# A hybrid encoder block on one core: a chain of constant products ahead of the first loop, and nine gate stores moved to another DMA queue

## The chip, the core and the metric

The kernel runs on one core of a Trainium2 chip. The metric is the device time of one execution in microseconds (us), as the median of several runs. The core has five engines that run side by side and wait for each other through semaphores: TensorE (PE in the profile; PEld is its weight load), VectorE (DVE), ScalarE (ACT), GpSimd (POOL) and SyncE (SP). Here SP does nothing but issue DMA transfers; ACT and POOL issue some too. Each engine takes its instructions strictly in the order in which the program lists them, so an instruction that waits holds up everything behind it on its engine.

## What is computed

One layer of a streaming encoder, in float32, for 16 meta tokens and 1024 positions of width 1024:

```python
xn = rmsnorm(h, norm_mix_g)
q, k, v, f_logit, u, gates = split(xn @ w_in)          # widths 512, 512, 512, 8, 512, 2048
y_a = forgetting_attention(q, k, v, f_logit) @ w_attn_out
z = gelu(s5(u))                                        # complex diagonal state-space model, 32 groups
zg = z @ w_glu
y_s = zg[..., :1024] * sigmoid(zg[..., 1024:])
g = sigmoid(gates)
h = h + (g[..., :1024] * y_a + g[..., 1024:] * y_s) @ w_o
h = h + conv_ffn(rmsnorm(h, norm_ffn_g))               # 1024 -> 5632 -> conv width 3 -> gated -> 1024
out = rmsnorm(h, norm_final_g)[16:]
```

## The kernel before

Every large product is made of three products of a reduced-precision format: each operand is cut into a high part (a cast, `hi`) and a low part (the rest, `lo`), and hi*hi, lo*hi and hi*lo are summed in one PSUM bank. A weight chunk therefore goes through a load (`raw`), a cast on ACT (`whi`) and a low part, which for the gate chunks is made by an ACT copy of the negated high part and a POOL DMA that adds the original to it in place (`wlo`, line 144).

The part of the program that matters here is its first 200 us:

1. **The first loop** (lines 405 to 413). The 1040 positions are cut into four blocks of 272, 256, 256 and 256. For block 0 the features (`xa` to `xhi`, `xlo`, lines 383 and 384) and the weights of `u` (`uraw` to `uh`, `ul`, lines 409 and 137) arrive in six pieces; as each arrives, TensorE adds its products to four PSUM banks, one for each 128 columns of `u`: 8 x 4 x 3 = 96 matmuls of 128x272 in all, on lines 351 to 353. The banks come from a ring of three called `mm` and a single one called `po`, so that the fifth product asked for, the first of block 1, gets the bank of the first:

```python
def mm_ps():
    mm_n[0] += 1
    if mm_n[1] and mm_n[0] % 4 == 0:
        return po_ps()
    return pp.tile([P, 512], F, tag="mm", name="mm", bufs=3)
```

   It is free once ACT has copied the first product out (line 421). Blocks 1 to 3 follow, 96 matmuls of 128x256 each.
2. **The state-space stage**, about 60 to 180 us. `u` is written to DRAM in another layout (`u_d`, line 455, 32 stores on SP's and POOL's queues) and read back by quarters (`U`, line 1910: quarters 0 and 1 on SP's queue, 2 and 3 on ACT's). For each quarter: tables `Vm` and `Gm` on DVE; transposes of `Vm` into `Wi` (PE line 1903, copied by ACT on line 1904); the input products `Wi` x `U` (PE line 1916, copied to `wr` and `wi` by eight ACT copies on lines 1919 and 1920); a scan on DVE into `St`; small products `Kt` (PE line 1879, ACT line 1881), spread to `Tm` by eight SP transfers (line 1889); the output products with `St` and `Tm` (PE lines 1957 and 1959), which ACT copies to `Y` (line 1960). There are two buffers for `U`, so that the load of quarter 3 follows the output products of quarter 1.
3. **The gate chunks**, in the same stretch. Eight chunks of 128 gate channels (i = 8 to 15, KD is 8), each in three pieces of 342 positions of 24 matmuls of 128x342 (lines 170 to 172), fill TensorE between the steps of the state-space stage. Below, 9.2 is the third piece (2) of chunk 9. ACT makes each piece a sigmoid (`gs`, line 505) and the piece is stored to DRAM (`g_d`, line 506). Chunk 8 has a buffer of its own (`g0s`); the others take turns in two buffers, so the sigmoid of a piece waits until the store of the piece two before it has landed:

```python
if i == KD:
    gs = g0s[:, t:t + n]
else:
    gs = pl.tile([P, LQ // 3], F, tag="gs", name="gs", bufs=2)
S.activation(gs, ps[:, :n], AF.Sigmoid)
GP.dma_start(g_d[P * i:P * i + P, t:t + n], gs)
```

   The stores stand on POOL's queue, in line with the loads of the gate weights and the `wlo` transfers. Since the buffers lie where `usb` (the rows of `u`) lay, the first sigmoid of chunk 9 also waits for the `u_d` stores.

Behind these stages come the key and query projections, the gated linear unit, the attention, the output projection and the feed-forward network, to 1440 us.

The order of instructions on each engine isn't written by hand: the code lists the steps, and a scheduler orders them when the program is built, by a model of their durations. An instruction added anywhere shifts that model's clock, and with it the order of independent steps behind it.

Of the kernel before, what the change touches and what calls it, by code (L numbers as in the profile page):

```python
# [9 lines left out]
F = mybir.dt.float32  # L10
# [9 lines left out]
P = 128  # L20
D = 1024
KD = D // P
# [22 lines left out]
UN = UBLK[0][1]  # L45
# [13 lines left out]
def block_kernel(ctx, tc, x, meta, xbt, x0t, g1t, w_q, w_k, w_v, w_f, w_u, w_g, b_f, w_ao, lam_d, bw_d, cw_d,  # L59
# [5 lines left out]
    V, S, GP, PE, SY = nc.vector, nc.scalar, nc.gpsimd, nc.tensor, nc.sync  # L65
# [13 lines left out]
# [5 lines that stand above are left out]
# [13 lines left out]
    def t_ps(name="tp"):  # L97
        return pp.tile([P, 512], F, tag="tp", name=name, bufs=2)
# [10 lines left out]
    g_d = dp.tile([2 * D, LQ], F, name="g_d")  # L109
# [36 lines left out]
    def wchunk(src, k, eng=None, act=False, copy=False):  # L146
        raw = wp.tile([P, k, P], F, tag="raw", name="raw", padded_shape=[P, KD, P])
        ld = (GP if act else SY).dma_start(raw, src)
        if act:
            after(ld, late[0])  # L150
        hi = wp.tile([P, k, P], R, tag="whi", name="whi", padded_shape=[P, KD, P])
        lo = wp.tile([P, k, P], R, tag="wlo", name="wlo", padded_shape=[P, KD, P])
        if act:
            cast = S.copy(hi, raw)
            if n_act[0]:
                after(cast, late[1])
            n_act[0] += 1
            lo_by_dma(lo, hi, src)
            return hi, lo
        if copy:  # L160
            S.copy(hi, raw)
            split_lo(V, lo, raw, hi)
            return hi, lo
        GP.tensor_scalar(hi, raw, 1.0, 0.0, ALU.mult, ALU.add)
        split_lo(eng or V, lo, raw, hi)
        return hi, lo

    def dense_steps(ps, whi, wlo, ahi, alo, k):
        for i in range(k):
            yield PE.matmul(ps, whi[:, i, :], ahi[:, i], start=(i == 0), stop=False)  # L170
            yield PE.matmul(ps, whi[:, i, :], alo[:, i], start=False, stop=False)  # L171
            yield PE.matmul(ps, wlo[:, i, :], ahi[:, i], start=False, stop=(i == k - 1))  # L172
# [126 lines left out]
    uraw = [wp.tile([P, 2, SW], F, tag="raw", name="uraw") for _ in range(2)]  # L299
    uraw += [sp.tile([P, 2, SW], F, tag="Tm", name="uraw", bufs=2) for _ in range(2)]  # L300
    uh = [wp.tile([P, 2, SW], R, tag=tag, name="uh") for tag in ("whi", "wlo") for _ in range(2)]
    xm = sp.tile([META, D], F, tag="tq", name="xm", bufs=3)

    xT = {0: [sp.tile([P, 4, UN], F, tag="tq", name="xa", bufs=3) for _ in range(2)]}
# [185 lines left out]
    def gate_chunk(i, pl, tanh):  # L490
        whi, wlo = gate0[1:] if i == KD else wchunk(w_g[i], KD, GP, act=not tanh)
        if tanh:
            gs = pl.tile([P, LQ], F, tag="gs", name="gs", bufs=1)
        for t, n in QBLK[::-1] if i == KD else QBLK:
            ps = mm_ps()
            yield from dense_steps(ps[:, :n], whi, wlo, xhi[:, :, T0 + t:T0 + t + n],
                                   xlo[:, :, T0 + t:T0 + t + n], KD)
            if tanh:
                S.activation(gs[:, t:t + n], ps[:, :n], AF.Tanh, scale=0.5)
# [3 lines that stand above are left out]
                else:  # L503
                    gs = pl.tile([P, LQ // 3], F, tag="gs", name="gs", bufs=2)
                S.activation(gs, ps[:, :n], AF.Sigmoid)
                GP.dma_start(g_d[P * i:P * i + P, t:t + n], gs)
        if tanh:
            GP.tensor_scalar(gs, gs, 0.5, 0.5, ALU.mult, ALU.add)
            if pl is not gp_ and i == KD - 1:
                okeep["g"] = gs  # L510
            else:
                SY.dma_start(g_d[P * i:P * i + P], gs)

    def stage_gates():
        for i in range(KD, 2 * KD):
            yield from gate_chunk(i, gp_, False)
# [412 lines left out]
    for pr in range(H // 2):  # L929
# [11 lines left out]
        for i in range(done, done + GA[pr]):  # L941
            gens.append(gate_chunk(i, ap, True))
            cnt += GAN
# [121 lines left out]
    for mm in gate_chunk(KD - 1, mg, True):  # L1065
        tc.add_manual_dep(mm.ins, marks[-1].ins.name, mybir.DependencyInfo(
            mybir.DependencyClass.NoSync, mybir.DependencyReason.DATA), reason="reserve")
# [959 lines left out]
```

## Time and profile before

| | us |
|---|---|
| Median of 3 runs | 1443.2 (1442.69 to 1445.39) |
| The profiled execution, time | 1445.58 |
| Its span in the trace | 1443.8 |
| TensorE busy in the span | 1422.4 (99%) |
| DVE, ACT, POOL busy | 1074.5, 722.4, 766.9 |
| Bytes moved by DMA | 214.06 MB |

The profile gives times from the start of the span. In a row of the timeline stand the start, the duration, the engine, the line, the operation, and output<-input with shapes; in brackets the idle time before it and what ended that. In a row of the waits stand the waiting instruction, what it waited for, and the total, the number and the longest of the waits. In a row of the windows stand the stretch, its length, and for each engine its busy time with the number of instructions. A busy TensorE isn't one at full speed: a matmul that is issued at half the rate still counts as busy.

### The profile page before, as it was taken

What the parts mean: (1) busy time and instruction counts of PE and PEld (TensorE: products, weight loads), DVE (VectorE), ACT (ScalarE), POOL (GpSimd) and SP (SyncE); (2) the same over time, 40 slices, a digit from 0 to 9 for tenths busy, and PEclk for the clock granted to TensorE, in tenths of its full rate; (3) what the DMA queues carried; (4) which work ended last, traced back from release to release, by engine and by line L of the source; (5) the groups of instructions that cost most, each with busy time, mean ns of one, the idle gap of its engine ahead of it and who ended that gap; (6) DMA issues with size and microseconds to landing.
All of it is one profiled execution on the core that took longest, in us unless ns stands there. A gap on an engine that the chain in (4) does not pass through costs nothing. (4 is left out here: it accounts for less than half of the span.)

```text
span 1443.8 us, 26609 instructions
## 1 busy us (share of the span) xinstructions
PE 1422.4 (99%) x9655; PEld 1346.2 (93%) x9655; DVE 1074.5 (74%) x2203; ACT 722.4 (50%) x1419; POOL 766.9 (53%) x887
## 2 busy tenths in 40 slices
PE   8999999999999999999999999999999999999997
PEld 8999999988999999999879999999999999887886
DVE  7999788843657676656469987788877776788875
ACT  7646585423646565533646444444444445643433
POOL 2642258632456556415861335555555544887794
PEclk9999999999999999999999999999999999999999
DMA  8675644521147422167964156667753327964333
GB/s 297 177 180 164 156 108 148 154 96 30 38 139 162 123 63 71 41 230 245 261 154 138 63 132 173 170 166 186 190 139 112 99 79 253 330 203 145 111 87 117
DMA packets 92968, 214.06 MB, mean 148 GB/s; under 512 B 15090, under 2 KB 22898, under 8 KB 92452
## 3 DMA queue, kind: packets, MB, share of 16 engines
q1 hardware_dynamic: 73124, 166.32, 35.0%
q0 software_dynamic: 17696, 41.29, 15.0%
q10 hardware_dynamic: 2016, 4.74, 0.9%
q8 instruction: 76, 1.25, 0.4%
q14 instruction: 56, 0.46, 0.1%
HBM read 170.88 MB, written 71.71 MB: 168 GB/s over the span
## 5 line engine op out<-in xcount | busy, mean ns | idle before, releaser
L170 PE MATMUL mm<-xhi,whi 128*128 128x342 f32 (+2 forms) x480 | 156.9, 327 | 1.3 <-DVE q L137 1.0
L172 PE MATMUL mm<-xhi,wlo 128*128 128x342 f32 (+2 forms) x480 | 155.3, 324 | 0.0
L171 PE MATMUL mm<-xlo,whi 128*128 128x342 f32 (+2 forms) x480 | 155.2, 324 | 0.0
L1183 POOL TENSOR_TENSOR ov<-ov,og 128x1024 f32<-128x1024 f32 x21 | 50.8, 2419 | 118.2 <-ACT og L1182 115.9
L137 DVE TENSOR_TENSOR sw<-sf,sw 128x512 fp32r<-128x512 f32 x72 | 74.2, 1031 | 46.2 <-ACT sw L1174 45.2
L1174 ACT CAST sw<-sf 128x512 fp32r<-128x512 f32 x72 | 44.9, 623 | 109.0 <-POOL sf L1321 80.2
L170 PEld LDWEIGHTS mm<-xhi,whi 128*128 128x128 f32 x480 | 90.5, 188 | 2.7 <-PE sp L818 0.8
L172 PEld LDWEIGHTS mm<-xhi,wlo 128*128 128x128 f32 x480 | 90.3, 188 | 0.6 <-issue 0.2
L171 PEld LDWEIGHTS mm<-xlo,whi 128*128 128x128 f32 x480 | 90.4, 188 | 0.2
L867 ACT CAST th<-tp 128x256 fp32r<-128x256 f32 (+3 forms) x120 | 56.2, 472 | 61.5 <-PE tp L860 29.3
L137 DVE TENSOR_TENSOR tl<-tp,th 128x256 fp32r<-128x256 f32 (+3 forms) x120 | 65.1, 547 | 25.7 <-ACT th L867 24.2
L1321 POOL TENSOR_TENSOR sf<-raw,sf 128x512 f32<-128x512 f32 x36 | 62.5, 1736 | 38.6 <-DVE sw L137 38.5
L1321 POOL TENSOR_TENSOR sf<-raw 128x512 f32<-128x512 f32 x36 | 48.5, 1348 | 62.2 <-DVE sw L137 23.4
L234 PE MATMUL mm<-xhi,sw 128*128 128x258 f32 (+1 forms) x288 | 81.0, 281 | 0.0
L232 PE MATMUL mm<-xhi,sw 128*128 128x258 f32 (+1 forms) x288 | 80.8, 280 | 0.0
L233 PE MATMUL mm<-xlo,sw 128*128 128x258 f32 (+1 forms) x288 | 80.7, 280 | 0.0
L832 POOL TENSOR_SCALAR pt<-pt,nm 128x144 f32<-128x144 f32 (+4 forms) x72 | 52.5, 742 | 49.3 <-DVE nm L831 48.2
L1373 DVE SCALAR_TENSOR_TENSOR ov<-hv,cwt,ov 128x1024 f32<-128x1024 f32 x36 | 69.0, 1918 | 0.4 <-ACT ov L1371 0.4
L1174 ACT CAST sw<-raw 128x512 fp32r<-128x512 f32 x70 | 43.0, 620 | 47.7 <-PE sp L234 23.9
L830 ACT ACTIVATE pt<-pt,nm 128x144 f32<-128x144 f32 (+4 forms) x72 | 52.9, 736 | 26.8 <-DVE nm L829 26.4
L823 DVE CUSTOM_DVE_ANT_0 pt<-sp,fb 128x328 f32<-128x328 f32 (+8 forms) x112 | 46.4, 430 | 20.1 <-PE sp L818 11.3
L137 DVE TENSOR_TENSOR sw<-raw,sw 128x512 fp32r<-128x512 f32 x70 | 57.4, 823 | 4.9 <-ACT sw L1174 4.7
(722 smaller groups left out, 5726.9 us busy)
## 6 DMA issues: line engine op xcount, KB each, us to landing
raw<-in_w_up_dram SPq DMA_DIRECT2D x44, 512.0 KB, 3.7
t_d<-in_w_dn_dram POOLq DMA_DIRECT2D x44, 256.0 KB, 6.9
wr<-t_d SPq DMA_DIRECT2D x44, 256.0 KB, 3.7
ar<-a_d SPq DMA_DIRECT2D x41, 256.0 KB, 5.1
a_d<-ov SPq DMA_DIRECT2D x18, 512.0 KB, 2.6
wr<-in_w_dn_dram SPq DMA_DIRECT2D x33, 256.0 KB, 3.7
t_d<-in_w_dn_dram SPq DMA_DIRECT2D x22, 256.0 KB, 4.4
t_d<-t_d SPq DMA_DIRECT2D x22, 256.0 KB, 4.8
```

The costliest lines, as they stand in the source:

```text
L137: return eng.tensor_tensor(out_, src, hi.bitcast(F), ALU.subtract)
L170: yield PE.matmul(ps, whi[:, i, :], ahi[:, i], start=(i == 0), stop=False)
L171: yield PE.matmul(ps, whi[:, i, :], alo[:, i], start=False, stop=False)
L172: yield PE.matmul(ps, wlo[:, i, :], ahi[:, i], start=False, stop=(i == k - 1))
L232: PE.matmul(ps, a[0][:, i], bh, start=(i == 0 and not joins), stop=False, skip_group_check=True)
L233: PE.matmul(ps, a[0][:, i], bl, start=False, stop=False, skip_group_check=True)
L234: PE.matmul(ps, a[1][:, i], bh, start=False, stop=(i == kh - 1), skip_group_check=True)
L830: S.activation(pt[:n, :kc], pt[:n, :kc], AF.Exp, bias=nm[:n, 1:2], scale=0.125, accum_out=nm[:n, 2:3])
L867: S.copy(th[:kn, z:tw], tp[:kn, z:tw])
L1174: S.copy(hi, src)
L1321: sums.append(GP.tensor_tensor(f_, a, b, op))
L1373: V.scalar_tensor_tensor(out=o, in0=h_[:, j:SEQ + j], scalar=cwc(j, m), in1=o, op0=ALU.mult, op1=ALU.add)
```

## The change

Two edits. First, ahead of the loads, DVE fills 128x272 numbers of a weight buffer that isn't needed yet (`uh[3]`, the last of the four `uh` buffers) with ones, and TensorE multiplies that tile by itself 17 times, into a PSUM bank of the ring `tp`. Nothing reads the result. The buffer's later writer, the cast of the last `uraw` piece, waits for these products. Second, the stores of chunks 8, 9 and 10, nine pieces, are issued by SP and no longer by POOL.

```diff
     uh = [wp.tile([P, 2, SW], R, tag=tag, name="uh") for tag in ("whi", "wlo") for _ in range(2)]
+    V.memset(uh[3].bitcast(F)[:, 0, :UN], 1.0)
+    busy = t_ps("busy")
+    for _ in range(17):
+        PE.matmul(busy[:, :UN], uh[3][:, 0, :P], uh[3][:, 0, :UN], start=True, stop=True)
     xm = sp.tile([META, D], F, tag="tq", name="xm", bufs=3)
...
                 S.activation(gs, ps[:, :n], AF.Sigmoid)
-                GP.dma_start(g_d[P * i:P * i + P, t:t + n], gs)
+                (SY if i < KD + 3 else GP).dma_start(g_d[P * i:P * i + P, t:t + n], gs)
```

Line numbers behind 301 are higher by 4 in the changed kernel. The order of the instructions differs from the first loop on to the forget gate's products (lines 537 and 538 before, 180 to 190 us); behind them it is the same on all engines.

SP's queue, from the stores of `u_d` on. Before:

```order
L455 DMA u_d<-usb 16x8x130 x16
L1910 DMA U<-u_d 128x1040 x2
L1889 DMA Tm<-Kt 16x1024
L1889 DMA Tm<-Kt 16x8x112
L1889 DMA Tm<-Kt 16x8x96
```

Now:

```order
L459 DMA u_d<-usb 16x8x130 x16
L1914 DMA U<-u_d 128x1040
L510 DMA g_d<-g0s 128x342 x3
L1914 DMA U<-u_d 128x1040
L510 DMA g_d<-gs 128x342 x6
L1893 DMA Tm<-Kt 16x1024
L1893 DMA Tm<-Kt 16x8x112
```

The load of `U` for quarter 1 stands behind the three stores of chunk 8, and the first `Tm` transfers stand behind the six stores of chunks 9 and 10.

ACT around the first quarter's input tables, with `gs` the sigmoids of pieces 9.2, 10.0 and 10.1 (the sigmoids of 9.0 and 9.1 stand just ahead in both). Before, from the low part of chunk 11's weights on:

```order
L143 ACTIVATE wlo<-whi 128x1024
L1904 COPY Wi<-sp 128x512
L1904 COPY Wi<-tp 128x512
L1919 COPY wr<-sp 64x260
L1920 COPY wi<-sp 64x260
L1919 COPY wr<-tp 64x260
L1920 COPY wi<-tp 64x260
L1919 COPY wr<-sp 64x260
L1920 COPY wi<-sp 64x260
L1919 COPY wr<-tp 64x260
L1920 COPY wi<-tp 64x260
L505 ACTIVATE gs<-mm 128x342
```

Now, from the cast of chunk 11's weights on:

```order
L154 CAST whi<-raw 128x1024
L509 ACTIVATE gs<-mm 128x342
L143 ACTIVATE wlo<-whi 128x1024
L509 ACTIVATE gs<-mm 128x342
L1908 COPY Wi<-sp 128x512
L1908 COPY Wi<-tp 128x512
L509 ACTIVATE gs<-po 128x342
L1923 COPY wr<-sp 64x260
```

The sigmoid of 9.2, which stood behind the eight copies of `wr` and `wi`, now stands ahead of the two copies of `Wi`, with the sigmoid of 10.0; that of 10.1 stands ahead of the copies of `wr`.

ACT ahead of the load of `U` for quarter 3. Before, from the last input copies of quarter 2 on, to that load:

```order
L1919 COPY wr<-sp 64x260
L1920 COPY wi<-sp 64x260
L1881 COPY Kt<-tp 16x512
L1881 COPY Kt<-sp 16x512
L154 CAST whi<-raw 128x1024
L505 ACTIVATE gs<-mm 128x342
L143 ACTIVATE wlo<-whi 128x1024
L1960 COPY Y<-tp 128x390
L1960 COPY Y<-sp 128x390
L1960 COPY Y<-tp 128x260
L1910 DMA U<-u_d 128x1040
```

Now, from the cast of chunk 14's weights on (a sigmoid, the copies of `Kt` and `Y` and then the load follow):

```order
L154 CAST whi<-raw 128x1024
L509 ACTIVATE gs<-mm 128x342
L143 ACTIVATE wlo<-whi 128x1024
L1923 COPY wr<-tp 64x260
L1924 COPY wi<-tp 64x260
L1923 COPY wr<-sp 64x260
L1924 COPY wi<-sp 64x260
L1923 COPY wr<-tp 64x260
L1924 COPY wi<-tp 64x260
L1923 COPY wr<-sp 64x260
L1924 COPY wi<-sp 64x260
```

The cast and the low part of chunk 14's weights, behind which POOL issues the `wlo` transfer, moved from just ahead of the load to ahead of quarter 2's eight input copies. On TensorE, between the output products of quarter 1 and the input products of quarter 3 stood 48 gate steps and 8 transposes, and now 37 and 8.

## The prediction

> **What bounds the kernel now.** I read the page's busy times first, then what TensorE waited for, then the stretches of the head.
>
> ```profile
> PE 1422.4 (99%) x9655; PEld 1346.2 (93%) x9655; DVE 1074.5 (74%) x2203; ACT 722.4 (50%) x1419; POOL 766.9 (53%) x887
> ```
>
> TensorE is busy for 99% of the span, so time can only go where it stands idle or runs slowly, and a new wait of TensorE costs its full length. Of all that it waited for, three rows lie in the part whose order the change touches:
>
> ```profile
> PE mm L351 <- ACT uh L409: 5.1, 1, 5.1
> PE mm L170 <- DVE q L137: 1.0, 2, 0.5
> PE sp L1916 <- DMA U<-u_d: 0.7, 1, 0.7
> ```
>
> The first is the start: TensorE has nothing until the first weights are cast at 5.08. The third is the input products of quarter 3, which wait for their `U`. Slow running shows in the windows of TensorE alone:
>
> ```profile
> 5.08:10.36 5.28, 5.28 (x23) 1.00 0.96 324
> 10.36:19.60 9.24, 9.24 (x75) 1.00 1.02 381
> 60.00:80.00 20.00, 20.00 (x129) 1.00 0.91 192
> ```
>
> In the first loop, 23 matmuls take 5.28 us (0.230 each) up to 10.36, and behind it 75 of the same form take 9.24 (0.123 each), though the column of the granted clock says 1.00 in both rows. So the first matmuls run at about half the rate, and that costs 23 x (0.230 - 0.123) = 2.5 us. The third row gives a gate step: 20.0 / 129 = 0.155 us. All that the change could win in its reach is these 2.5 us, 0.7 for `U` and 1.0 for the projection: 4.2 us, or 0.29% of 1443.2. I count a difference as one beyond 0.2%, 2.9 us, about what a measurement of this kernel can tell from no change.
>
> **The head.** The chain lies in the idle 5.08 us. Its fill of 272 columns on DVE has no row of its own; a fill of 32 columns and a two-input operation on 272 columns bound it, 0.09 and 0.50 us.
>
> ```profile
> 1.24 0.09 DVE L1760 MEMSET sm<- 128x32 f32 x1
> 3.61 0.50 DVE L384 SCALAR_TENSOR_TENSOR xlo<-xa,g1T,xhi 128x272 fp32r<-128x272 f32 x1 [2.25 <-ACT xhi L383]
> ```
>
> DVE idles between these two, so the fill hides there, and the chain can start between 1.0 and 1.5 us. At the slow rate it takes 17 x 0.230 = 3.9 us, to 4.9 to 5.4: it hardly delays the first true product. What follows then runs at the fast rate within some microseconds. How much of the 2.5 us survives is decided by what is late next. In the first loop that is the data, and behind it a PSUM bank:
>
> ```profile
> 13.46 1.05 ACT L409 CAST uh<-uraw 128x1024 fp32r<-128x1024 f32 x1
> 15.78 3.31 ACT L383 ACTIVATE xhi<-xT,g1T 128x256 fp32r<-128x256 f32 x8 [1.27 <-DMA xT<-in_xbt_dram]
> 19.00 0.36 ACT L421 COPY usb<-mm 128x272 f32<-128x272 f32 x1
> 19.60 0.28 PE L351 MATMUL mm<-xhi,uh 128*128 128x256 f32 x1
> ```
>
> The last weights are cast at 13.46 + 1.05 = 14.5, and the 24 products of that piece take 24 x 0.123 = 3.0, so the loop can end at 17.5 to 18.5 instead of 19.6. But the first product of block 1 needs the bank that ACT empties at 19.00 to 19.36, and this copy stands on ACT behind the eight features of block 1, which start when their load lands (1.27 us of waiting ahead of 15.78). The changed order keeps eight features, then copy, and moves no load. So block 1 can start at 19.4 and not at 18; TensorE idles 1 us that it used to spend on slow matmuls. **The head gives 19.6 - 19.4 = 0.2 us.** If the copy weren't in the way, it would give up to 2.5.
>
> The Trainium skill, in TensorE: Matmul & The Clock Gate, Part 1, says that TensorE's clock starts at half rate and is let go after a window of about 3.4 us of steady work. The trace agrees in kind, with 5.28 us from the first matmul to the fast rate. By that rule alone one would book the whole 2.5 us; that is the first rival.
>
> **The stores on SP.** Nine issues leave POOL, which isn't waited for by TensorE in this stretch; that alone gives nothing. Two things that they are moved past on SP: the load of `U` for quarter 1 goes out three issues later, and is used only behind the first quarter's products; the first `Tm` transfers go out behind the sixth store, and wait for tables that in the new order come later than that piece. I cost both at nothing. The price is on ACT, where the sigmoid of 9.2 now stands ahead of the copies of `Wi`. It needs the store of 9.0 landed.
>
> ```profile
> 75.76 1.92 SPq L1910 DMA_DIRECT2D U<-u_d  x2
> 61.81 13.85 SPq L455 DMA_DIRECT2D u_d<-usb  x16
> 74.98 0.46 ACT L505 ACTIVATE gs<-po 128x342 f32<-128x342 f32 x1 [7.18 <-DMA u_d<-usb]
> 83.98 0.59 ACT L1904 COPY Wi<-sp 128x512 f32<-128x512 f32 x1 [4.24 <-PE sp L1903]
> 87.49 0.61 PE L1916 MATMUL sp<-U,Wi 128*128 128x130 f32 x4
> ```
>
> The order of issue on SP is `U`, three stores, `U`, store of 9.0. A `U` takes 1.92 / 2 = 0.96; a store between half of that and 13.85 / 16 = 0.87. The store of 9.0 goes out at 75.76 + 2 x 0.96 + 3 x (0.48 to 0.87) = 79.1 to 80.3. How long do stores take here? The answers for line 506 in the windows 80 to 82, 76 to 82 and 90 to 98 end so:
>
> ```profile
> DMA to landing us min/median/max: 6.1/6.3/6.4
> DMA to landing us min/median/max: 6.1/6.4/8.5
> DMA to landing us min/median/max: 3.4/5.6/6.7
> ```
>
> What ACT then does has these lengths, by the rows of before:
>
> ```profile
> 88.14 0.37 ACT L1919 COPY wr<-sp 64x260 f32<-64x260 f32 x1 [3.08 <-PE sp L1916]
> 92.55 0.46 ACT L505 ACTIVATE gs<-mm 128x342 f32<-128x342 f32 x1
> 92.89 0.56 ACT L1881 COPY Kt<-sp 16x512 f32<-16x512 f32 x1
> 93.36 1.06 ACT L143 ACTIVATE wlo<-whi 128x1024 fp32r<-128x1024 f32 x1
> 94.33 0.56 ACT L1881 COPY Kt<-tp 16x512 f32<-16x512 f32 x1
> ```
>
> With 6.3 it lands at T = 85.4 to 86.6 (with 3.4 at 82.5, with 8.5 at 88.8). From T on ACT does a sigmoid, a `wlo` copy, another sigmoid and the first copy of `Wi`, which with the distances between these starts (0.34 behind the sigmoid, 0.97 behind `wlo`, 0.34 again) and the 0.59 of `Wi` takes 2.3 us in round numbers. TensorE's first input product, at 87.49 before and 0.2 earlier now, then waits for T + 2.3 - 87.3 = T - 85.0: 0.4 to 1.6 us, zero at the low end of T, 3.8 at the high end. I take 0.9, since 6.3 is the row of the same stores at the same time. The sigmoid of 10.1 ahead of the `wr` copies waits for the store of 9.2 in the same way and may cost a further 0 to 1.3; I take 0.4, as the later window has stores of 3.4. **In sum +1.3 us.** The cover of the rest: the scan of the last quarter ends on DVE at 171.2 and is used at 175.85, so a chain that slips by these 1 to 3 us makes nobody wait.
>
> ```profile
> 169.77 1.42 DVE L1639 TENSOR_TENSOR St<-ta,wr 64x516 f32<-64x516 f32 x2
> 175.85 0.39 PE L1957 MATMUL tp<-St,Gm 128*128 128x130 f32 x2
> ```
>
> The Trainium skill, in DMA: Bandwidth & Descriptors, Issuing engines are not separate DMA queues, says that transfers from SP, ACT and POOL share the same 16 DMA engines, and another issuer saves issue time only. That speaks against a gain from this edit; no row here shows a plain store of this size from SP, and by the page T stays where the landing times of before put it, as I took it.
>
> **The load of `U` for quarter 3.** It took 8.9 us before, and its sister for quarter 2 took 5.2 (the answers for line 1910 in 125 to 140 and 100 to 120):
>
> ```profile
> 132.98 0.35 ACTq L1910 DMA_DIRECT2D U<-u_d  x1
> DMA to landing us min/median/max: 8.9/8.9/8.9
> 131.89 0.90 POOL L144 DMA_DIRECT2D wlo<-in_w_g_dram  x1 [0.23 <-ACT wlo L143]
> 114.32 0.33 ACTq L1910 DMA_DIRECT2D U<-u_d  x1
> DMA to landing us min/median/max: 5.2/5.2/5.2
> 110.58 0.90 POOL L144 DMA_DIRECT2D wlo<-in_w_g_dram  x1 [0.36 <-ACT wlo L143]
> ```
>
> The slow one left 1.1 us behind a `wlo` transfer of half a megabyte, the quick one 3.7 us behind. In the new order the cast that leads to the `wlo` transfer stands eight copies (8 x 0.37 = 3 us) and more ahead of the load. But TensorE now has 11 gate steps less to do in between: 11 x 0.155 = 1.7 us less cover. At 8.9 us the wait would be 0.7 + 1.7 = 2.4; at 5.2 it is gone. The order is that of the quick one, so I take none: **-0.7 us**, and keep +1.7 as the other end.
>
> **Sum.** -0.2 + 1.3 - 0.7 = +0.4 us. The profiled execution would go from 1445.58 to 1446.0; it lies 2.4 above the median of the runs, 1443.2, which goes to **1443.6**. The wait of the projection (1.0) stays: its cause, DVE, is untouched.
>
> **Rivals.**
> - *The whole warm-up survives* (0.11). Block 1's bank or its load is ready earlier than the trace of before shows. Then -2.5 - 0.7 = -3.2 and no wait for stores: 1440.0, faster by 0.22%. Against it: the copy's place on ACT and the load that precedes it.
> - *ACT stands at the sigmoid of 9.2* (0.16). The store of 9.0 takes 8.5 us as the longest of that stretch did, T is 88.8: 3.8 us of waiting, then 1.3 for 10.1, less 0.9: 1443.2 + 4.2 = 1447.4, slower by 0.3%. It costs from T = 85.0 on, and decides from 87.5. For it: the new load of `U` and three more stores stand ahead on the same queue. Against: before, POOL's stores in that stretch mostly took 6.3.
> - *`U` of quarter 3 is late again* (0.14): +1.7 for -0.7, 1446.0, within 0.2%.
> - *The chain doesn't lift the rate* (0.05): products of constants might not count, or the phase is unlucky. Then the head is 0 to 0.3 slower, 1444.0, no difference.
>
> The forecast has 0.50, with a range of its own from 1442.3 to 1445.0; 0.04 is for a wait that I don't see, of either sign. Faster by over 0.2%: 0.11 + 0.02 = 0.13. Slower: 0.16 + 0.02, and 0.02 of the third rival: 0.20. The rest, 0.67, is within. The range reaches from the first rival, 1440.0, to just past the third, 1446.4, and leaves out the second.
>
> **What would show it.** In the changed profile: 17 matmuls from about 1.3 us, the fast rate from 6 to 8 us, TensorE idle for about 1 us before block 1, and block 1 at 19.4. If block 1 starts at 18.5 or earlier, the step on the bank is wrong. The sigmoid of 9.2 waits for the store of 9.0 until 85 to 87, and the first input product waits up to 2 us; if it starts at 87.3, that term is 0. The row of `U` for quarter 3 lands within 6 us, and TensorE doesn't wait for it. Any other wait of TensorE over 1 us before 200 us makes the sum wrong.

## The result, and the profile after

The changed kernel takes 1453.7 us (median of 6 runs, 1452.6 to 1460.1) beside 1444.2 for the kernel before in the same comparison: a ratio of 1.0068, 95% interval 1.0053 to 1.0083. That is some 9.8 us slower by the ratio, and 9.5 between the medians. The forecast was 1443.6, with 1446.4 as the upper end of its range. The profiled executions are 8.0 us apart in their spans, 1451.8 and 1443.8. Near the end, where the order is the same, TensorE waits for the `hs` of DVE: twice in the profiled run before (1.9 and 1.8 us), once in that after (1.9). Six of the fourteen profiled runs of this document have two such waits and eight have one, with the change and without, so this is luck of the run.

What TensorE waited for between 60 and 230 us, in the waits of the changed kernel:

```profile
PE sp L1920 <- ACT Wi L1908: 3.9, 1, 3.9
PE mm L170 <- DVE fg L548: 3.5, 1, 3.5
PE mm L232 <- ACT c L241: 0.7, 1, 0.7
```

The wait for `U` is gone, as forecast, and these three stand in its place. The first is the second rival of the prediction. The other two were in none of its rivals.

**The head.** TensorE's and ACT's rows of the timeline:

```profile
1.24 3.98 PE L305 MATMUL busy<-uh 128*128 128x272 f32 x17 [1.24 <-DVE uh L302]
5.50 0.40 PE L355 MATMUL mm<-xhi,uh 128*128 128x272 f32 x1 [0.28 <-ACT uh L413]
14.51 3.33 ACT L387 ACTIVATE xhi<-xT,g1T 128x256 fp32r<-128x256 f32 x8 [0.73 <-DMA xT<-in_xbt_dram]
17.99 0.29 PE L357 MATMUL po<-xhi,ul 128*128 128x272 f32 x1
18.17 0.39 PE L355 MATMUL mm<-xhi,uh 128*128 128x256 f32 x1
```

The chain runs from 1.24 for 4.0 us. The first true product starts at 5.50 instead of 5.08, but at the fast rate at once, and block 1 starts at 18.17 instead of 19.60.

**The first wait.** ACT's row of instructions:

```profile
76.29 1.05 ACT L154 CAST whi<-raw 128x1024 fp32r<-128x1024 f32 x1 [2.35 <-PE mm L171]
88.19 0.46 ACT L509 ACTIVATE gs<-mm 128x342 f32<-128x342 f32 x1 [10.85 <-DMA g_d<-gs]
88.54 1.05 ACT L143 ACTIVATE wlo<-whi 128x1024 fp32r<-128x1024 f32 x1
89.49 0.45 ACT L509 ACTIVATE gs<-mm 128x342 f32<-128x342 f32 x1
89.83 0.59 ACT L1908 COPY Wi<-sp 128x512 f32<-128x512 f32 x1
90.29 0.61 ACT L1908 COPY Wi<-tp 128x512 f32<-128x512 f32 x1
```

ACT stood for 10.85 us at the sigmoid of 9.2, until the store of 9.0 had landed. That store went out on SP at 79.68 and took this long (the answer for line 510 there):

```profile
DMA to landing us min/median/max: 8.4/8.4/8.4
```

The windows of TensorE over both waits, with the stretches behind them:

```profile
86.24:90.47 4.23, 0.29 (x3) 0.96 0.18 61
90.47:93.54 3.07, 3.07 (x14) 0.50 0.83 100
196.95:202.77 5.82, 5.82 (x18) 0.50 0.28 36
```

The fourth column is the granted clock. After each wait TensorE ran at half rate, for 3.1 and 5.8 us. The Trainium skill, in TensorE: Matmul & The Clock Gate, HAM oscillation, warns of idle gaps beyond about 3.4 us, behind which the clock is halved; here gaps of 4.2 and 3.6 us did that, and other runs show it behind gaps of 1.9 to 2.7 us as well (last section), so that this bound is no safe one here. The prediction left it out.

**The second wait.** The output products of quarter 2, TensorE's row before and after:

```profile
161.91 0.38 PE L1957 MATMUL sp<-St,Gm 128*128 128x130 f32 x2
169.80 0.39 PE L1961 MATMUL sp<-St,Gm 128*128 128x130 f32 x2
```

They come 7.9 us later. Their `Y` goes to DRAM and is read back by eight loads (`zt`, line 645), for the z differences on DVE. Here are POOL's `wlo` transfer for the key weights, and DVE's rows:

```profile
183.32 0.91 POOL L144 DMA_DIRECT2D wlo<-in_w_k_dram  x1 [0.41 <-ACT wlo L143]
191.88 1.30 DVE L667 TENSOR_TENSOR zf<-zt,zf 128x520 f32<-128x520 f32 x1 [9.19 <-DMA raw<-in_w_glu_dram]
196.41 0.48 DVE L548 SCALAR_TENSOR_TENSOR fg<-mm,bf,fg 8x272 f32<-8x272 f32 x1
```

The same two rows of DVE before:

```profile
181.67 1.30 DVE L663 TENSOR_TENSOR zf<-zt,zf 128x520 f32<-128x520 f32 x1 [6.47 <-DMA raw<-in_w_glu_dram]
188.35 0.48 DVE L544 SCALAR_TENSOR_TENSOR fg<-mm,bf,fg 8x272 f32<-8x272 f32 x1
```

The bracket of 191.88 names a load of the gated unit's weights, the next transfer on the same queue. That can't be what DVE waited for: it went out at 185.1 at the earliest and took over 8 us. The `zt` loads fit. Here are the answers for before (all eight), for after in 181 to 183.2 (the first five), and for after in 183.2 to 185 (the last four, one of them counted twice), and for the weight load:

```profile
DMA to landing us min/median/max: 2.8/3.7/4.6
DMA to landing us min/median/max: 2.4/3.1/3.7
DMA to landing us min/median/max: 3.5/7.3/7.3
DMA to landing us min/median/max: 8.3/8.4/8.5
```

The loads that went out behind the `wlo` transfer took 7.3 us instead of 3.1, and the last landed at 191.8. DVE, which had been idle for 9.19 us, then did the differences, and the forget gate's sum stood behind them at 196.41; ACT's share of that sum stood behind a cast of the same differences. TensorE needed the sum's bank at 193.3.

### The profile page after: what moved, and what is told of

It reads as the page before. It is cut to its first block, busy times and chain, and to the rows that moved or that the text cites. A ratio compares the mean times of both kernels' runs of the same rounds, so it can differ in the third digit from the quotient of the medians.

```text
span 1451.8 us, 26650 instructions
## 1 busy us (share of the span) xinstructions
PE 1428.6 (98%) x9672; PEld 1351.9 (93%) x9672; DVE 1079.3 (74%) x2204; ACT 721.6 (50%) x1419; POOL 759.6 (52%) x878
## 3 DMA queue, kind: packets, MB, share of 16 engines
q0 software_dynamic: 17120, 39.72, 14.4%
## 5 line engine op out<-in xcount | busy, mean ns | idle before, releaser
L137 DVE TENSOR_TENSOR sw<-sf,sw 128x512 fp32r<-128x512 f32 x72 | 79.3, 1101 | 49.5 <-ACT sw L1178 49.5
```

Source lines behind the costliest of these rows:

```text
L137: return eng.tensor_tensor(out_, src, hi.bitcast(F), ALU.subtract)
```

## The experiments

To compare kernels, the late time of a stretch is used: for each matmul, the distance to the next one's start less the usual distance (the lower quartile) of its form, summed over the stretch. It counts waits and half rate together. Times are those of the profiled run; each ratio is that of the comparison with the kernel before, which ran beside it. In the edits, `after(a, b)` holds the instruction a behind b in the order, and `...` stands for lines left out; the lines that only collect instructions in lists (`w_in_copies`, `u_loads` and others) are left out too.

| kernel | ACT starts block 1's features, us | block 1 starts on TensorE, us | late, 86 to 100 us | late, 180 to 230 us | ratio to before (95%) |
|---|---|---|---|---|---|
| before | 15.78 | 19.60 | 0.6 | 1.1 | |
| changed | 14.51 | 18.17 | 6.0 | 7.8 | 1.0068 (1.0053 to 1.0083) |
| E1 constant products alone | 15.50 | 19.12 | 1.0 | 0.8 | 0.9992 (0.9981 to 1.0003) |
| E2 stores alone | 15.45 | 19.31 | 5.5 | 7.1 | 1.0056 (1.0039 to 1.0072) |
| E3 sigmoid of 9.2 behind | 15.89 | 19.52 | 0.6 | 1.8 | 0.9990 (0.9979 to 1.0000) |
| E4 forget sum ahead | 14.87 | 18.86 | 5.0 | 4.6 | 1.0041 (1.0026 to 1.0056) |
| E5 `U` behind the stores | 17.11 | 20.73 | 4.3 | 7.1 | 1.0048 (1.0031 to 1.0065) |
| E6 fillers | 15.51 | 19.15 | 5.2 | 5.9 | 1.0069 (1.0051 to 1.0087) |
| E7 order, stores on POOL | 14.39 | 18.38 | 3.3 | 7.7 | 1.0050 (1.0031 to 1.0069) |
| E8 bank of `tp` | 15.76 | 19.39 | 0.4 | 0.9 | 0.9989 (0.9977 to 1.0000) |
| E9 stores of chunk 9 read another tile | 15.54 | 19.17 | 0.4 | 5.5 | 1.0027 (1.0016 to 1.0038) |
| E10 bank of `sp` | 14.85 | 18.69 | 1.6 | 2.2 | 1.0006 (0.9997 to 1.0015) |
| E11 quarter 2's products later | 15.78 | 19.41 | 1.0 | 1.1 | 1.0013 (1.0004 to 1.0022) |
| E12 `wlo` behind the read-back | 14.53 | 18.50 | 6.9 | 4.1 | 1.0048 (1.0033 to 1.0063) |

### Which edit, and is it the queue or the order?

**E1**, the constant products alone:

```diff
-                (SY if i < KD + 3 else GP).dma_start(g_d[P * i:P * i + P, t:t + n], gs)
+                GP.dma_start(g_d[P * i:P * i + P, t:t + n], gs)
```

> The 17 constant products as in the changed kernel, all gate stores on POOL's queue as before. The order in the state-space stage is nearly that of before. Theory (the loss of 9.5 us is all in the stores' edit, by the order that came with it): block 1 starts near 18.2 us as in the changed kernel (1.4 us gained), no wait for Wi, the wait for U of quarter 3 stays at 0.7 to 1.0, so 1444.2 - 1.4 = 1442.8. Rival (the constant products shift the order enough to carry part of the loss): waits of TensorE between 80 and 200 us grow and the time is 1446 or more.

The ratio is 0.9992: the loss isn't there, nor can the gain be told from nothing. Block 1 didn't start near 18.2 but at 19.12, behind a wait for the bank:

```profile
18.16 0.29 PE L357 MATMUL po<-xhi,ul 128*128 128x272 f32 x1
19.12 0.39 PE L355 MATMUL mm<-xhi,uh 128*128 128x256 f32 x1 [0.67 <-ACT usb L425]
```

**E2**, the stores alone:

```diff
-    V.memset(uh[3].bitcast(F)[:, 0, :UN], 1.0)
-    busy = t_ps("busy")
-    for _ in range(17):
-        PE.matmul(busy[:, :UN], uh[3][:, 0, :P], uh[3][:, 0, :UN], start=True, stop=True)
```

> The nine stores on SP, no constant products. The order in the state-space stage is that of the changed kernel. Theory: both waits of the changed kernel (3.9 us for Wi, 3.5 us for the forget gate's sums) with the half clock behind each are there, and the head's 1.4 us aren't gained: 1453.7 + 1.4 = 1455.1. Rival (it takes both edits, the chain's earlier head makes the stores collide): the waits shrink, 1444 to 1448.

Both waits are there (3.2 us for `Wi`, 3.6 in two for the forget gate's sums), and the ratio is 1.0056. The loss belongs to the stores' edit.

**E3**, both edits, with the sigmoid of 9.2 where it stood before:

```diff
-                    S.copy(wi[64 * e:64 * e + 64, q:q + 2], w3[64:])
+                    w_in_copies.append(S.copy(wi[64 * e:64 * e + 64, q:q + 2], w3[64:]))
...
-                S.activation(gs, ps[:, :n], AF.Sigmoid)
+                sg = S.activation(gs, ps[:, :n], AF.Sigmoid)
+                if (i, t) == (KD + 1, QBLK[2][0]):
+                    after(sg, w_in_copies[3])
```

> Both edits, and the sigmoid of 9.2 held behind the first quarter's input copies, where it stood before; the rest of the order follows it back to nearly that of before. Theory (the order makes the loss, not the queue): the wait for Wi and the wait for the forget gate's sums are both gone, the time is 1444.2 - 1.4 = 1442.8, within 1.5. Rival (SP's queue makes it: the stores land 2 us later there, and ACT or the weight loads behind it pay anyway): 1447 or more, with a wait of TensorE of over 2 us between 80 and 110 us.

The stores are still on SP, and the store of 9.0 landed later than in any other run; the loss is gone all the same. Its landing time, and what TensorE waited for from 60 to 230 us:

```profile
DMA to landing us min/median/max: 13.2/13.2/13.2
```

```profile
PE mm L171 <- DVE fg L551: 0.7, 1, 0.7
PE sp L1926 <- ACT Wi L1914: 0.6, 1, 0.6
```

A store that takes 13.2 us costs nothing where nobody waits, and one that takes 8.4 costs several us with TensorE's inputs behind its sigmoid. So it is the order that came with the queue, not the queue. The Trainium skill, in DMA: Bandwidth & Descriptors, Issuing engines are not separate DMA queues, has it that another issuer saves issue time and nothing else; E3 agrees, at 0.9990 beside the 0.9992 of E1.

**E7**, the other side of it: all stores on POOL, but the sigmoid ahead of `Wi`:

```diff
-                S.copy(Wi[:, 4 * q:4 * q + 4].rearrange("p g m -> p (g m)"), wt)
+                table_copies.append(S.copy(Wi[:, 4 * q:4 * q + 4].rearrange("p g m -> p (g m)"), wt))
...
+                if (i, t) == (KD + 1, QBLK[2][0]):
+                    for c_ in table_copies[:2]:
+                        after(c_, sg)
```

> The constant products, all stores on POOL as before, but the sigmoid of 9.2 held ahead of the two copies of Wi, as in the changed kernel; the rest of the order follows it to within a few places of the changed kernel's. Theory (the order makes the loss, not the queue): the store of 9.0 lands near 87.2 on POOL's queue too, ACT stands there until then, TensorE waits some 3 us for Wi and again for the forget gate's sums: 1450 to 1454. Rival (POOL's queue lands the stores in time): 1443 to 1446.

The ratio of 1.0050 is that of the theory, but the first wait isn't its mechanism. ACT's rows, and TensorE's wait:

```profile
88.53 1.04 ACT L155 CAST whi<-raw 128x1024 fp32r<-128x1024 f32 x1 [10.02 <-PE mm L172]
89.60 1.06 ACT L144 ACTIVATE wlo<-whi 128x1024 fp32r<-128x1024 f32 x1
90.56 0.44 ACT L510 ACTIVATE gs<-mm 128x342 f32<-128x342 f32 x1
90.90 0.58 ACT L1915 COPY Wi<-sp 128x512 f32<-128x512 f32 x1
```

```profile
PE mm L171 <- ACT gs L510: 2.4, 1, 2.4
```

In this order the cast of the next weights had slipped ahead of the sigmoid too. ACT stood at that cast until 88.53, for products of TensorE and not for a store: the store of 9.0, issued at 79.12, had landed 7.3 us later, at 86.4. The sigmoid stood behind the cast and its `wlo` copy, and TensorE ran into it as a gate product that waited for the sigmoid's bank; it did not wait for `Wi`. So the sigmoid's wait for its store isn't tested here. What holds is that the order costs with the stores on POOL as well, and that the second loss comes in full (7.7) without SP, with quarter 2's output products behind the same 539 gate steps as in the changed kernel.

### The first wait

**E9** takes the reason for it away and leaves the order of TensorE, ACT, DVE and POOL as it is:

```diff
-                (SY if i < KD + 3 else GP).dma_start(g_d[P * i:P * i + P, t:t + n], gs)
+                src = xhi[:, 0, t:t + n].bitcast(F) if i == KD + 1 else gs
+                (SY if i < KD + 3 else GP).dma_start(g_d[P * i:P * i + P, t:t + n], src)
```

> Both edits; the three stores of chunk 9 read a tile that is long there (high parts of the features) instead of the sigmoid's buffer, so that no sigmoid waits for them; what they write to DRAM is not the gate then. The order is the changed kernel's on every engine. Theory (both waits come from the order; the first delays TensorE and the state-space chain alike and so can't cause the second): the wait for Wi goes with the half clock behind it, 4.1 + 1.3 us, and the waits at 180 to 230 us stay at 7 to 8 us in all: 1453.7 - 5.4 = 1448.3. Rival (the second wait is the echo of the first): both go, 1443, as fast as with the sigmoid held behind.

On SP the order isn't the changed kernel's, against what was expected: the three stores of chunk 9, which no longer follow a sigmoid, go out at 35.3 to 56.4 us, ahead of the stores of `u_d`. The median is 1448.35, the theory's number. TensorE's waits from 60 to 230 us, all of them:

```profile
PE mm L170 <- DVE fg L549: 2.9, 2, 1.8
PE mm L232 <- ACT c L241: 1.3, 1, 1.3
```

The first wait is gone and the second stays, 5.5 us late in all. The ratio falls from 1.0068 to 1.0027, 0.0041 or 5.9 us, but not all of that is the first wait. In the traces the first stretch loses 5.6 us of its late time, which is the wait with the half rate behind it, and the second stretch a good 2, while block 1 starts 1.0 us later; that the theory's number came out is in part luck. The second wait doesn't need the first, but is smaller without it.

**E5** asks why the store of 9.0 took 8.4 us. One instruction moves on SP:

```diff
+                if (i, t) == (KD + 1, QBLK[1][0]):
+                    after(u_loads[1], st)
```

> Both edits; on SP the load of U for quarter 1 goes out behind the stores of 9.0 and 9.1 and no longer ahead of them. Nothing else in the order moves. Theory (the store of 9.0 lands late because half a megabyte stands ahead of it on its own queue): it goes out near 78.3 and lands at 85 to 86 instead of 88.1, the wait for Wi shrinks from 3.9 to 1 or 2 us, the half clock behind it goes, and the forget gate's wait shrinks with it: 1449 to 1451. Rival (the 16 engines are simply full, with the weight load that POOL now issues 5.7 us earlier): the store still lands at 87.5 or later, the wait is 3 us or more, 1453 to 1455.

Without the load of `U` ahead of it the store took 7.4 us, and the wait for `Wi` was 2.0. The store's landing time, and ACT's row of the sigmoid of 9.2:

```profile
DMA to landing us min/median/max: 7.4/7.4/7.4
88.76 0.46 ACT L510 ACTIVATE gs<-mm 128x342 f32<-128x342 f32 x1 [8.89 <-DMA g_d<-gs]
```

But in this run the load of block 1's features landed late, so that TensorE and the store, which went out at 81.3, were late as well: the sigmoid of 9.2 starts at 88.76, later than the changed kernel's 88.19. The wait for `Wi` is shorter because TensorE came later, not because the store landed sooner. The time, 1.0048, has an interval that overlaps that of the changed kernel, and the second wait stayed at 7.1. So E5 doesn't tell what the load of `U` costs. The traces of the other runs say that it can't be much: behind that load the same store took 7.7 to 8.9 us (the changed kernel, E2, E4, E6 and E12; in E3 13.2), and on POOL's queue 6.2 to 8.4 (before, E1, E7, E8, E10 and E11). How much of the 8.4 us is the queue and how much the traffic (POOL's next weight load went out at 77.64 instead of 83.35, since no stores stood ahead of it) isn't settled.

### The second wait

**E4** moves only the forget gate's first sums ahead of the z differences, on ACT and DVE:

```diff
+            if k == 0:
+                after(d2, fg_log[0][1])
...
+                if k == 0 and t_ is not T1:
+                    after(c_, fg_log[0][0])
```

> Both edits, and on DVE and ACT the first sums of the forget gate held ahead of the second z difference and its cast (line 667 and 672); nothing else in the order moves. Theory: the second wait (3.5 us) is only DVE and ACT standing in line behind that difference, so it goes, with the half clock behind it (6.8 us at half, worth 2.4 here): 1453.7 - 5.9 = 1447.8, and the first wait stays at 3.9. Rival (the state-space stage itself is 8 us late, so the gated unit's products wait for it instead): a new wait of some us at 210 to 230 us, 1452 or more.

The late time fell from 7.8 to 4.6, half of what the theory gave: the next sum and the gated unit's first products then waited.

```profile
PE mm L170 <- DVE fg L550: 1.7, 1, 1.7
PE mm L232 <- ACT c L241: 1.3, 1, 1.3
```

So it isn't only a matter of standing in line; the differences themselves are late. Not all of the 3.2 us need be the edit's, either: in this run only one of the eight `zt` loads went out behind the `wlo` transfer (three in the changed kernel's), and the last landed at 189.1 instead of 191.8. The interval of the ratio overlaps that of the changed kernel.

**E6** fills the wait with matmuls that nobody needs:

```diff
+                if (w, pr, t) == (0, 0, BLK[1][0]):
+                    fill_ps = t_ps("fill")
+                    for _ in range(20):
+                        after(PE.matmul(fill_ps[:, :342], whi[:, 0], xhi[:, 0, :342], start=True, stop=True), step)
```

> Both edits; 20 matmuls of 128x342 into a spare bank, which nobody reads, stand on TensorE just ahead of the product that waits for the forget gate's sums (a wait of 3.7 us, then 5.8 us at half rate). Nothing else in the order moves. Theory (the half rate behind the wait comes from TensorE's idling and costs 2.9 us of its own): the fillers take 20 x 0.155 = 3.1 us out of the wait, the granted clock stays at 1.00 there, and the time falls by 2.5 to 2.9 to 1451. Rival (the rate behind the wait has another cause, or the fillers only push the work out): 1453.7 or more.

The clock stayed up, and nothing was won. The windows:

```profile
197.00:201.00 4.00, 3.91 (x22) 1.00 0.45 50
201.00:204.00 3.00, 0.56 (x5) 1.00 0.01 3
```

TensorE got ahead at full rate, and then stood for 2.4 us at the next sum. The ratio is 1.0069; the 3.1 us of the fillers themselves aren't in the table's late time. Here the half rate filled time in which TensorE would have waited anyway; DVE's chain sets the end of this stretch.

**E11** puts one thing of the changed order into E1: the place of quarter 2's output products, behind 539 of the 576 gate steps instead of 508 (510 before).

```diff
+    for qt, m in y_mm:
+        if qt == 2:
+            after(m, gate_log[538])
```

> The constant products alone (stores on POOL, no sigmoid moved, no wait for Wi), and one thing of the changed kernel's order: the output products of quarter 2 stand behind 539 of the 576 gate steps on TensorE instead of 508. Theory (the second wait comes from that place: with 31 steps x 0.155 = 4.8 us less work between these products and the products that need the forget gate's sums, the trip of quarter 2 through DRAM to the z differences is no longer covered): the waits at 180 to 230 us grow from 0.8 to 5 or 6 us in all and the time is 1.0025 of before, near 1449. Rival (it needs the late scans of the whole chain): the waits stay below 2 us and the time is 0.9992 of before.

In the trace my theory fell: these products came at 167.2, 5 us late, and TensorE's longest wait from 60 to 230 us was this:

```profile
PE tp L1927 <- ACT Wi L1915: 0.5, 1, 0.5
```

The place alone need not make the wait. In this trace all eight `zt` loads were out by 180.2, and the `wlo` transfer followed at 180.3; the last load landed at 183.5. But the profiled run is the fastest of the eleven, 1443.85 us beside a median of 1446.42, and the ratio, 1.0013, is 0.0021 above that of E1 and lies between the two expectations. With the transfer so close behind the last load it may have cut in in other runs; no trace shows that, and what those 3 us are isn't known.

**E12** tries what that points to: in the changed kernel, the `wlo` transfer behind the read-back.

```diff
+        if hold:
+            after(neg, hold[0])
+            after(add, hold[1])
+            after(hold[2], add)
+            after(hold[3], neg)
...
+            hold[:] = ssm_outs[6:8] + z_log[:2] if (w, pr) == (1, 0) else []
```

`neg` is ACT's copy and `add` the transfer; the first two lines hold them behind quarter 3's Gelu and `y_d` store, the next two keep a z difference on POOL and a cast on ACT behind them.

> Both edits; the low part of the key weights (ACT's copy and POOL's wlo transfer of half a megabyte, line 144) stands behind quarter 3's Gelu and its y_d store, some 4 us later, so that it goes out behind the eight loads that read quarter 2 back (zt, line 645) and not between them. The order is otherwise the changed kernel's, but for a few places on ACT and DVE behind it. Theory (quarter 2's products stand so late that this transfer overtakes the end of its read-back: the three loads behind it took 7 us, those ahead 2.5 to 4): the last zt lands at 188 instead of 191.8, the z difference (line 667) starts there, the waits at 180 to 230 us fall from 7.8 to 4 and the time from 1453.7 to 1450; the first wait stays. Rival (quarter 2 is late, and nothing else matters): zt still lands at 191, 1453.7.

The eight loads now took 2.2 to 4.1 us, the last landed at 188.5, and TensorE's waits are two:

```profile
DMA to landing us min/median/max: 2.2/3.5/4.1
```

```profile
PE sp L1932 <- ACT Wi L1920: 3.6, 1, 3.6
PE mm L175 <- DVE fg L553: 1.9, 1, 1.9
```

The late time of the second stretch is 4.1, as expected. The ratio fell to 1.0048, that is by 2.9 us beside the 3.7 expected, though its interval overlaps that of the changed kernel; the trace shows the gain, the time only suggests it. So the second wait has two parts. Quarter 2 is late, by its place in the order and by the first wait, and what is left here, 4.1 beside 1.1 before, is the price of that without the transfer. And the lateness makes the transfer of half a megabyte, which used to follow the read-back, cut into it, for the other 3.7 us. E9 agrees: there one load alone went out behind the transfer (at 178.14, the transfer at 178.13), and it took 6.4 us; the others took 2.3 to 4.0, as far as the trace tells.

### The bank

**E8** and **E10** give block 1's first product another bank, with the constant products alone:

```diff
+        if (b, m) == (1, 0):
+            mm_n[0] += 1
+            ps = s_ps()
+        else:
+            ps = mm_ps()
...
+            if b == 1 and k == 0 and ends:
+                after(head_mm, ends[-1])
```

This is E10; E8 has `t_ps()` in place of `s_ps()`, and not the last two lines, which keep block 1's products in order behind block 0.

> The constant products alone (stores on POOL), and block 1's first product in a bank of the ring tp, so that it needn't wait until ACT has copied block 0's first bank out. The order in the head and the state-space stage shifts a little with it. Theory (with the clock up early, that bank is what is late next): block 1 starts at 18.1 to 18.5 instead of 19.1 and the time is 0.7 below that of the constant products alone, 0.9985 of before. Rival (the features of block 1 or the last weights are late anyway): block 1 starts at 19 or later and nothing changes, 0.9992.

> The constant products alone (stores on POOL), and block 1's first product in a bank of the ring sp, first in TensorE's order behind block 0, so that it needs no bank that ACT empties. (The run with the bank of tp left a product first that still took a bank of mm.) Theory (that bank, free 3.6 us after the features' load lands, is what is late next): block 1 starts within 0.3 us of the end of block 0, at 18.0 to 18.6, and the time is 0.7 below that of the constant products alone: 0.9985 of before. Rival (the features are late as well): block 1 starts at 19 or later, 0.9992.

In E8 the order put a product with a bank of `mm` first, which waited 0.9 us for ACT's copy, so it tells nothing of the bank. In E10 block 1 follows block 0 with no gap:

```profile
18.56 0.29 PE L357 MATMUL po<-xhi,ul 128*128 128x272 f32 x1
18.69 0.28 PE L355 MATMUL sp<-xhi,uh 128*128 128x256 f32 x1
```

But block 0 ended 0.4 us later than in E1, and ACT started block 1's features at 14.85, so that by the 3.6 us of the other runs the old bank would have been free at 18.5 as well. So neither run shows what another bank gains; that the bank is late next is shown by E1's wait for ACT's copy. The time doesn't gain either (1.0006): the order behind had moved again, with 1.2 us of new waits at the forget gate's sums and 1.1 at `Wi`. No version was found that is faster than the kernel before beyond the measurement: E1, E3 and E8 lie 0.0008 to 0.0011 below it, each with an interval that reaches to 1.0000 or past it.

## Why the prediction was wrong, step by step

- **The head's mechanism was right.** A gain of 0.2 us was forecast, with block 1's bank as the next limit. The profiled run gained 1.4, which is luck: the load of block 1's features landed 1.3 us earlier than in the run before. By the prediction's own sign, block 1 at 18.5 or earlier, the step on the bank would be wrong; the other runs show that it stands. In E1, E5, E8, E9, E11 and E3 block 1 starts 3.62 or 3.63 us after ACT starts its features, as long as eight features and a copy take, and that start moves between 14.4 and 17.1 from run to run. Over the eleven profiled runs with the chain, E10 left aside, block 1 starts at 19.1 on average, against 19.60 and 19.31 in the two without it, a gain of about 0.3. The fast rate was there at the first product, at 5.5, and not at 6 to 8.
- **The load of `U` for quarter 3 was right**: 4.2 us to land, and no wait.
- **The stores' term was mis-sized**: +1.3 was forecast, and the first stretch lost 5.4. The formula held: the store of 9.0 went out at 79.68 (79.1 to 80.3 was forecast), and `Wi` followed 2.3 us behind its landing. I took 6.3 us for the landing, from POOL's stores in one trace; it took 8.4, which is the rival's 8.5. In the five other traces with these stores on POOL it took 6.2 to 8.4, so that 6.3 was at the low end even without the change of queue. TensorE, early by the head's gain, then waited 3.9 and not 0.9. The 0.4 for the sigmoid of 10.1 was nothing. The price of this rival should also have held the half rate: the 5.6 us that the first stretch loses in E9 are well above the wait. Even so the rival's 1447.4 would have been 6 us short.
- **The cover was wrong, and that cost most**: it was put at nothing, and the second stretch lost 6.7 us. "A chain that slips by these 1 to 3 us makes nobody wait" rested on the scan of the last quarter, 4.65 us ahead of its use. But quarter 2's products slipped by 7.9 us, 4.5 of them from the order alone (29 gate steps of 0.155), which could be counted beforehand; and the next user was not that quarter's scan but the way through DRAM to DVE, where the forget gate's sum stands in line. I followed the chain to the nearest use and stopped. Even the collision had its row in the prediction, in another place: a load behind a `wlo` transfer took 8.9 us instead of 5.2. The prediction named its own test, any other wait of TensorE over 1 us before 200 us, and the 3.5 us at 193 us were such a wait.
- **The sum.** In profiled spans: head -1.4, first wait with its half rate +5.4, `U` and small changes to 180 us -0.8, second stretch +6.7, the two late waits of the end -2.1, the rest +0.2: +8.0.

## What to carry to other kernels

When a scheduler moves the order, count for every long chain how many steps of the bottleneck engine now stand ahead of it and behind it, and follow it through every hop, DRAM and in-order queues included, to the engine that never waits. The queue of a transfer matters less than who stands behind the instruction that waits for it, and the landing time of a store in one trace is one sample of several. And a wait of TensorE is priced with the half rate behind it, unless another wait there would swallow that.

## What the runs showed of the hardware

- The chain of constant products moved the full clock from 10.4 and 9.7 us (the two profiled kernels without it) to between 4.6 and 7.2 (the twelve with it).
- A gap need not be long to halve the clock. TensorE's idle times of 2.7 us in E4 (for `Wi`), 2.0 in E5 (for `Wi`) and 1.9 in E12 (at 198.7) were each followed by 3.41 us at half clock, which began 0.7 to 1.2 us after the work had started again; 2.4, 3.2 and 2.5 us in E7 were followed by none. So the length of the gap alone doesn't decide it; what else does isn't settled. The half stretches inside the kernels lasted 3.41 or 6.83 us.
- A plain load of 65 KB took 7.3 us instead of 3.1 when it went out behind the half-megabyte `wlo` transfer, which adds to what is in place; with the transfer moved behind the loads (E12) the eight took 2.2 to 4.1.

The window of TensorE in E12 behind its gap of 1.9 us, with the granted clock in the fourth column:

```profile
200.62:206.00 5.38, 5.38 (x22) 0.68 0.29 98
```
